# Hyena's chain on the vector engine alone, and its transforms' first forward and last inverse level summed by TensorE in PSUM

## The chip, the cores and the metric

One core of one Trainium2 chip. The metric is the device time of one execution in microseconds; the kernel before took 2783.18 us, median of three runs (2772.97 to 2788.09).

## The reference

A two-layer trunk over 1,024 tokens of width 1,024 with 256 context tokens, everything in fp32. Layer 0 projects the normalised tokens once and gives the channels to two mixers beside each other: a Hyena operator (512 channels) and a differential attention (four heads); both are joined by one output projection. Layer 1 is a spatial-gating MLP. Each layer ends in a ConvFFN. The change lies in Hyena and, by one table, in the attention's rotary embedding:

```python
def fftconv_bidir(u, h_full, d_skip):
    uf = jnp.fft.rfft(uf32, n=2 * L, axis=1)
    hf = jnp.fft.rfft(h_full, n=2 * L, axis=0)
    y = jnp.fft.irfft(uf * hf[None], n=2 * L, axis=1)[:, :L]
...
    v, x1, x2 = jnp.split(proj, 3, axis=-1)
    z = v
    for o, gate in enumerate((x1, x2)):
        z = gate * fftconv_bidir(z, filt[:, o], d_skip[o])
```

So there are two long convolutions one after the other, each a transform, a product with the filter's spectrum and an inverse transform, and a gate behind it.

## The kernel before

`layer0_front` holds two generators that `eager` interleaves. `main` makes the projections, a tile of 128 channels by 1,024 tokens at a time: V (`proj_v`), the context's K (`proj_kc`), Hyena's twelve tiles with the short convolution (`proj_hyena`, `conv_mtile`), and the eight tiles of Q and K with their rotation (`proj_qk`). Each such tile is 48 fp32r products of 512 columns, from weights that are split into a rounded part (`whi`, ScalarE) and a rest (`wlo`, `wunit`); the table `F_W` says which engine makes the rest. `side` makes the filters' spectra (`filters`, `dft_part`, written to `Hd`) and then, for each half of 256 channels, the chain of `conv_chain`: for o = 0 and 1, `dft`, `spectrum`, `idft`, and the inverse products with the gate. That makes four rounds in a row; each needs the result of the one before it in its half, and the second half comes behind the first.

A round: `dft(z, n)` multiplies the eight residues of time (slots 0 to 7, in two groups of four) with cosine and sine tables (`tbf`) on TensorE; `fwd(z, c, g)` is four fp32 products of 256 columns into one two-bank PSUM tile (`pf`, two buffers). Group 1 is copied to SBUF by ScalarE (L437), then VectorE forms sum and difference with group 0 straight from PSUM (`a`, `b`). The other levels of the transform are additions of 256, 512 or 1,024 elements per partition in f8 tiles, and two scaled ones (`stt`). `spectrum` multiplies with the filter's spectra, loaded from `Hd` into h8 tiles by DMAs on ScalarE's queue (L314). `idft` adds up again, in place, into E and O, and its last level makes q0 and q1 from E plus and minus O. The inverse products with `tbi` follow: for o = 0, 16 products of 256 columns in two tiles, each multiplied by the gate x1 into the next z; for o = 1, 32 products of 128 columns, multiplied by x2 and stored to `yd`.

Which engine takes an addition is written in tables of letters, V for VectorE (DVE in the profile), G for GpSimd (POOL): `F_DFT` (18 letters a round), `F_INV` (25), `F_SP` (6 for each half spectrum), `F_ROPE` (4 for each Q or K tile: two multiplications, an addition, a subtraction), `F_PART` for the filters. `turns` deals them out in the program's order. The lines of all these additions are L132 (`binop`) and L128 (`stt`), so the profile's rows tell them apart by tile: f is an f8 tile, h a loaded spectrum or a late Q or K, t a t4 tile (a projection's result, four buffers), pj the projections' PSUM, pf Hyena's.

The order in which each engine's queue gets its instructions is set by the tile framework's scheduler when the program is built, from the program's order, priorities (`first()` puts evacuations ahead) and its own estimates. Each queue then runs in order, and an instruction that waits holds up those behind it.

Of the kernel before, what the change touches and what calls it, by code (L numbers as in the profile page):

```python
# [20 lines left out]
P = 128  # L21
# [16 lines left out]
UL, UP = (10, 8, 10), ((6,) * 7,) * 3  # L38
DL, DP = (1, 5, 4, 4, 5), ((3, 3, 3, 3, 3, 5, 8),) + ((3,) * 7,) * 4
BW, LW = 6, 2  # L40
F_DFT, F_INV = ("VGVGVVVGVVVGVGVVVG", "VGVGVVVGVVVGVGVVVG", "VGVGVVVGVVVGVGVVVG", "VGVGVVVGVVVGGGVVVG"), ("VGVVVVGGVGVVVGGGVVGVGVVGG", "VGVVVVGGVGVVVGGGVVGVGVVGG", "VGVVVVGGVGVVVGGGVVGVGVVGG", "VGVVVVGVVGVVVGGGVVGVGVVGG")
F_PART = ("VGGGVGGVVVVVG", "VGGVVGGVVVVVV", "VGGGVGGVVVVVG", "VGGVVGGVVVVVV", "VGGGVGGVVVVVG", "VGGVVGGVVVVVV", "VGGGVGGVVVVVG", "VGGVVGGVVVVVV")
F_SP = ("GGVVVV", "GGVVVV", "GGVVVV", "GGVVVV", "GGVVVV", "GGVVVV", "GGVVVV", "GGVVVV")
F_W = ("GGGGGGGGGGGG", "GGGG", "VGGG", "VGGVVGGG")
F_ROPE = ("GVVG", "GVVV", "GVVG", "VVVG", "GVVG", "GVVG", "GVVV", "GVGG")
F_H, F_X, F_SQ = "VGVVGVVG", "VVVVVVVV", ("V", "V", "V", "V", "V", "V", "V")
A_D = "GGGGGGGGGGGGGGGGGGGGGGGVGVGGVGGVV"
A_C = "VAV" * 4
# [22 lines left out]
RT2 = math.sqrt(0.5)  # L71
# [21 lines left out]
def tile_kernel(ctx: ExitStack, tc: tile.TileContext, ap: dict, out: bass.AP, stop=None):  # L93
# [194 lines left out]
    def layer0_front(fp):  # L288
        with ExitStack() as es:
# [141 lines left out]
            def dft(z, n):  # L431

                e = turns(F_DFT[n])
                a, b = f8(), f8()
                for c in range(2):
                    g1 = fwd(z, c, 1)
                    A.copy(out=b[:, c], in_=g1)  # L437
                    g0 = fwd(z, c, 0)
                    add(V, a[:, c], g0, b[:, c])
                    sub(V, b[:, c], g0, b[:, c])  # L440
                    yield
                cd = f8()
                add(e(), cd[:, :, 0:2], a[:, :, 0:2], a[:, :, 2:4])
                sub(e(), cd[:, :, 2:4], a[:, :, 0:2], a[:, :, 2:4])
                Xe = f8()
                add(e(), Xe[:, :, 0], cd[:, :, 0], cd[:, :, 1])
                sub(e(), Xe[:, :, 2], cd[:, :, 0], cd[:, :, 1])
                sub(e(), Xe[:, 0, 1], cd[:, 0, 2], cd[:, 1, 3])
                add(e(), Xe[:, 1, 1], cd[:, 1, 2], cd[:, 0, 3])
                add(e(), Xe[:, 0, 3], cd[:, 0, 2], cd[:, 1, 3])  # L450
                sub(e(), Xe[:, 1, 3], cd[:, 1, 2], cd[:, 0, 3])
                yield
                eu = f8()
                sub(e(), eu[:, 0, 0], b[:, 0, 0], b[:, 1, 2])
                add(e(), eu[:, 1, 0], b[:, 1, 0], b[:, 0, 2])
                add(e(), eu[:, 0, 1], b[:, 0, 0], b[:, 1, 2])
                sub(e(), eu[:, 1, 1], b[:, 1, 0], b[:, 0, 2])
                sub(e(), eu[:, :, 2], b[:, :, 1], b[:, :, 3])
                add(e(), eu[:, :, 3], b[:, :, 1], b[:, :, 3])
                uv = f8()  # L460
                sub(e(), uv[:, 0, 0], eu[:, 0, 2], eu[:, 1, 3])
                add(e(), uv[:, 1, 0], eu[:, 1, 2], eu[:, 0, 3])
                add(e(), uv[:, 0, 1], eu[:, 0, 2], eu[:, 1, 3])
                sub(e(), uv[:, 1, 1], eu[:, 1, 2], eu[:, 0, 3])
                Xo = f8()
                stt(V, Xo[:, :, 0:2], uv[:, :, 0:2], RT2, eu[:, :, 0:2], MUL, ADD)
                stt(V, Xo[:, :, 2:4], uv[:, :, 0:2], -RT2, eu[:, :, 0:2], MUL, ADD)
                return Xe, Xo
# [102 lines left out]

            def idft(Y, n):

                ye, yo = Y
                e = turns(F_INV[n])
                t = f8()
# [23 lines left out]
                sub(e(), O[:, 0, 3], d[:, 1, 1], d[:, 0, 1])  # L600
                stt(V, O[:, 1, 3], d[:, 0, 1], -1.0, d[:, 1, 1], MUL, SUB)
                yield
                q0, q1 = f8(), f8()
                add(e(), q0[:, :, 0], E[:, :, 0], O[:, :, 0])
                sub(e(), q1[:, :, 0], E[:, :, 0], O[:, :, 0])
                stt(V, q0[:, :, 1::2], O[:, :, 1::2], RT2, E[:, :, 1::2], MUL, ADD)
                stt(V, q1[:, :, 1::2], O[:, :, 1::2], -RT2, E[:, :, 1::2], MUL, ADD)
                add(e(), q0[:, 0, 2], E[:, 0, 2], O[:, 1, 2])
                sub(e(), q0[:, 1, 2], E[:, 1, 2], O[:, 0, 2])
                sub(e(), q1[:, 0, 2], E[:, 0, 2], O[:, 1, 2])  # L610
                add(e(), q1[:, 1, 2], E[:, 1, 2], O[:, 0, 2])
                return q0, q1

            def conv_chain(half):
                while half not in zs:
# [2 lines left out]
                for o in range(2):  # L618
# [7 lines left out]
                    if o == 0:  # L626
                        xg = h8(x1d[half].rearrange("p a b -> p (a b)"), (1, 8))[:, 0]
                        z = f8z()
                        for g in range(2):
                            ps = ps4()  # L630
                            for r in range(4):
                                for c in range(2):
                                    mm(ps[:, r], tbi[:, c, g * 4 + r], q[g][:, c, r], c == 0, c == 1)
                            gs = slice(g * 4, g * 4 + 4)
                            mul(V, z[:, gs], ps, xg[:, gs])
                            yield
                    else:
                        for j in range(2):
                            ps = ps2("pf")
                            for g in range(2):  # L640
                                for r in range(4):
                                    rs = slice((g * 4 + r) * P, (g * 4 + r + 1) * P)
                                    for c in range(2):
                                        mm(ps[:, rs], q[g][:, c, r, j * P : (j + 1) * P], tbi[:, c, g * 4 + r],
                                           c == 0, c == 1)
                            t = t4()
                            st(t, x2d[2 * half + j])
                            tv = t.rearrange("p (s r) -> p s r", r=8)
# [1225 lines left out]
```

## Time and profile before

| | us |
|---|---|
| median of three runs | 2783.18 |
| lowest, highest | 2772.97, 2788.09 |
| the profiled execution | 2781.85 |
| its span, first to last instruction | 2780.1 |
| TensorE busy (share of the span) | 2488.7 (90%) |
| VectorE busy | 1803.7 (65%) |
| GpSimd busy | 1264.8 (45%) |
| ScalarE busy | 1205.2 (43%) |

The profiled execution's own time is the span and 1.75 us around it. The shares are averages over stages that differ. Hyena's chain lies between 289 and 601 us of the span, attention begins at 663, and the rest of the network follows it. An fp32 product (the Hyena ones) appears as two records on TensorE; an fp32r product as one. Records of TensorE overlap in the timeline, so its pace is read from one start to the next.

### The profile page before, as it was taken

What the parts mean: (1) busy time and instruction counts of PE and PEld (TensorE: products, weight loads), DVE (VectorE), ACT (ScalarE), POOL (GpSimd) and SP (SyncE); (2) the same over time, 40 slices, a digit from 0 to 9 for tenths busy, and PEclk for the clock granted to TensorE, in tenths of its full rate; (3) what the DMA queues carried; (4) which work ended last, traced back from release to release, by engine and by line L of the source; (5) the groups of instructions that cost most, each with busy time, mean ns of one, the idle gap of its engine ahead of it and who ended that gap; (6) DMA issues with size and microseconds to landing.
All of it is one profiled execution on the core that took longest, in us unless ns stands there. A gap on an engine that the chain in (4) does not pass through costs nothing. (4 is left out here: it accounts for less than half of the span.)

```text
span 2780.1 us, 30586 instructions
## 1 busy us (share of the span) xinstructions
PE 2488.7 (90%) x11192; PEld 1981.5 (71%) x11192; DVE 1803.7 (65%) x2021; ACT 1205.2 (43%) x1871; POOL 1264.8 (45%) x917
## 2 busy tenths in 40 slices
PE   6799667767988889999999999999999999999897
PEld 2798556655767766777777777778877777787676
DVE  4676787874998376656666876642367665566854
ACT  2322111113767255555555444512257565665342
POOL 1333654545444163332323776613343433338775
PEclk9899888888999989999999999999999999999998
DMA  7134131235761265788878833311335777779422
GB/s 279 65 111 158 38 121 39 90 128 181 227 188 50 73 204 129 206 206 216 217 205 227 294 121 110 113 38 48 142 88 125 175 181 170 173 160 319 144 80 99
DMA packets 166855, 412.76 MB, mean 148 GB/s; under 512 B 16011, under 2 KB 28815, under 8 KB 164528
## 3 DMA queue, kind: packets, MB, share of 16 engines
q1 hardware_dynamic: 86352, 248.76, 27.9%
q0 software_dynamic: 34848, 63.45, 13.4%
q10 hardware_dynamic: 45504, 98.58, 9.6%
q8 instruction: 88, 1.44, 0.2%
q14 instruction: 63, 0.52, 0.1%
HBM read 261.31 MB, written 85.98 MB: 125 GB/s over the span
## 5 line engine op out<-in xcount | busy, mean ns | idle before, releaser
L154 PE MATMUL b<-u,u 128*128 128x512 f32 (+1 forms) x5624 | 1331.1, 396 | 65.2 <-POOL u L132 23.8
L154 PEld LDWEIGHTS b<-u,u 128*128 128x128 f32 x5624 | 1063.1, 192 | 331.4 <-POOL u L132 34.1
L132 DVE TENSOR_TENSOR u<-u,u 128x512 fp32r<-128x512 f32 (+2 forms) x470 | 464.5, 1014 | 337.9 <-ACT u L1141 178.9
L132 POOL TENSOR_TENSOR u<-u,u 128x512 fp32r<-128x512 f32 (+1 forms) x338 | 504.6, 1514 | 298.5 <-ACT u L1141 183.9
L1152 POOL DMA_DIRECT2D u<-u x242 | 211.3, 920 | 491.9 <-ACT u L1151 378.7
L1141 ACT CAST u<-u 128x512 fp32r<-128x512 f32 x462 | 261.7, 616 | 238.6 <-DVE u L132 96.0
L154 PE MATMUL b<-x,u 128*128 128x512 f32 x1224 | 296.8, 397 | 0.8 <-DMA u<-u 0.8
L128 DVE SCALAR_TENSOR_TENSOR u<-u,cols,u 128x1023 f32<-128x1023 f32 x176 | 232.3, 1326 | 93.2 <-ACT u L1588 85.2
L154 PEld LDWEIGHTS b<-x,u 128*128 128x128 f32 x1224 | 229.5, 188 | 61.9 <-issue 3.4
L132 POOL TENSOR_TENSOR f<-f 128x256 f32<-128x256 f32 (+2 forms) x99 | 124.7, 1273 | 209.9 <-DVE f L132 180.7
L1150 ACT CAST u<-u 128x512 fp32r<-128x512 f32 x242 | 146.1, 614 | 117.7 <-DVE u L132 89.6
L1151 ACT ACTIVATE u<-u 128x512 fp32r<-128x512 f32 x242 | 149.3, 628 | 67.2 <-POOL u L132 60.3
L132 DVE TENSOR_TENSOR f<-f 128x256 f32<-128x256 f32 (+3 forms) x176 | 177.2, 1055 | 1.1
L132 DVE TENSOR_TENSOR u<-u,b 128x512 f32<-128x512 f32 (+1 forms) x132 | 112.2, 859 | 71.5 <-PE b L154 66.7
L154 PE MATMUL pj<-hh,whi 128*128 128x512 f32 x320 | 132.7, 415 | 24.2 <-DVE t L128 14.0
L1588 ACT ACTIVATE u<-u,cols 128x1024 f32<-128x1024 f32 x88 | 109.3, 1242 | 90.2 <-DVE u L132 89.4
L128 DVE SCALAR_TENSOR_TENSOR x<-b,mods,x 128x512 f32<-128x512 f32 (+1 forms) x104 | 88.7, 905 | 68.4 <-PE b L154 68.4
L154 PE MATMUL pj<-hh,wlo 128*128 128x512 f32 x320 | 130.2, 407 | 3.2 <-POOL wlo L132 1.6
L154 PE MATMUL pj<-hl,whi 128*128 128x512 f32 x320 | 131.3, 410 | 0.0
L132 POOL TENSOR_TENSOR p<-p,p 128x1280 f32<-128x1280 f32 x27 | 79.4, 2944 | 94.1 <-ACT p L885 75.3
L874 ACT ACTIVATE p<-s,nx 128x1280 f32<-128x1280 f32 x64 | 85.0, 1328 | 42.0 <-DVE nx L870 39.2
L147 ACT CAST whi<-wraw 128x1024 fp32r<-128x1024 f32 x28 | 29.3, 1049 | 160.5 <-PE pj L154 138.5
(229 smaller groups left out, 3218.3 us busy)
## 6 DMA issues: line engine op xcount, KB each, us to landing
u<-u POOLq DMA_DIRECT2D x242, 256.0 KB, 4.6
u<-wup SPq DMA_DIRECT2D x88, 512.0 KB, 4.9
Td<-u ACTq DMA_DIRECT2D x66, 512.0 KB, 5.5
u<-Td SPq DMA_DIRECT2D x56, 512.0 KB, 4.4
wraw<-modw SPq DMA_DIRECT2D x48, 512.0 KB, 5.5
u<-wdown SPq DMA_DIRECT2D x40, 512.0 KB, 6.1
wraw<-modw0b SPq DMA_DIRECT2D x32, 512.0 KB, 4.6
xs<-x ACTq DMA_DIRECT2D x48, 256.0 KB, 2.0
```

The source lines that it names most:

```text
L128: eng.scalar_tensor_tensor(out=o, in0=a, scalar=sc, in1=b, op0=op0, op1=op1)
L132: eng.tensor_tensor(out=o, in0=a, in1=b, op=op)
L147: A.copy(out=hi, in_=x)
L154: T.matmul(o, l, r, start=st and not onto, stop=sp, skip_group_check=onto)
L874: A.activation(q.p[m], q.s, AF.Exp, bias=q.nx, accum_out=q.l[:, m : m + 1])
L1141: A.copy(out=t[:, H0], in_=x)
L1150: A.copy(out=t[:, H0], in_=x)
L1151: A.activation(t[:, H1], t[:, H0].bitcast(F32), AF.Copy, scale=-1.0)
L1152: G.dma_start(out=t[:, H1], in_=x, accum_op=ADD)
L1588: A.activation(a, c, AF.Identity, bias=col(f"fb{l}", f), scale=col(f"fw{l}1", f))
```

## The change

All letters of `F_DFT`, `F_INV`, `F_SP` and `F_ROPE` become V. The first level of `dft` is no longer made by VectorE: each sum and each difference of the two groups is accumulated in a PSUM tile by two products per residue, the difference with a copy of z's second group that ScalarE negates (`zn`, a t4 tile); ScalarE then copies all four tiles to SBUF. The last level of `idft` goes the same way: instead of q0 and q1 ScalarE makes a negated copy `n` of O (slots 1 and 3 scaled by the root of one half) and scales O's slots 1 and 3 in place, and each inverse product becomes two, one with E and one with O or n.

```diff
-F_DFT, F_INV = ("VGVGVVVGVVVGVGVVVG", ...
+F_DFT, F_INV = ("V" * 18,) * 4, ("V" * 25,) * 4
-F_SP = ("GGVVVV", ...
+F_SP = ("V" * 6,) * 8
-F_ROPE = ("GVVG", "GVVV", "GVVG", "VVVG", "GVVG", "GVVG", "GVVV", "GVGG")
+F_ROPE = ("VVVV",) * 8
...
                 a, b = f8(), f8()
+                zn = t4().rearrange("p (r n) -> p r n", r=4)
+                A.activation(zn, z[:, 4:8], AF.Copy, scale=-1.0)
                 for c in range(2):
-                    g1 = fwd(z, c, 1)
-                    A.copy(out=b[:, c], in_=g1)
-                    g0 = fwd(z, c, 0)
-                    add(V, a[:, c], g0, b[:, c])
-                    sub(V, b[:, c], g0, b[:, c])
+                    for o, z1 in ((a, z[:, 4:8]), (b, zn)):
+                        ps = ps4()
+                        for r in range(4):
+                            mm(ps[:, r], tbf[:, c, r], z[:, r], True, False)
+                            mm(ps[:, r], tbf[:, c, 4 + r], z1[:, r], False, True)
+                        A.copy(out=o[:, c], in_=ps)
...
-                q0, q1 = f8(), f8()
-                add(e(), q0[:, :, 0], E[:, :, 0], O[:, :, 0])
-                sub(e(), q1[:, :, 0], E[:, :, 0], O[:, :, 0])
-                stt(V, q0[:, :, 1::2], O[:, :, 1::2], RT2, E[:, :, 1::2], MUL, ADD)
-                stt(V, q1[:, :, 1::2], O[:, :, 1::2], -RT2, E[:, :, 1::2], MUL, ADD)
-                add(e(), q0[:, 0, 2], E[:, 0, 2], O[:, 1, 2])
-                sub(e(), q0[:, 1, 2], E[:, 1, 2], O[:, 0, 2])
-                sub(e(), q1[:, 0, 2], E[:, 0, 2], O[:, 1, 2])
-                add(e(), q1[:, 1, 2], E[:, 1, 2], O[:, 0, 2])
-                return q0, q1
+                n = f8()
+                for r, w in ((0, 1.0), (1, RT2)):
+                    A.activation(n[:, :, r::2], O[:, :, r::2], AF.Copy, scale=-w)
+                A.activation(O[:, :, 1::2], O[:, :, 1::2], AF.Copy, scale=RT2)
+
+                def terms(g, c, r):
+                    if r == 2:
+                        o = (O, n)[g ^ c][:, 1 - c, 2]
+                    else:
+                        o = (O, n)[g][:, c, r]
+                    return E[:, c, r], o
+
+                return terms
...
-                                    mm(ps[:, r], tbi[:, c, g * 4 + r], q[g][:, c, r], c == 0, c == 1)
+                                    for i, x in enumerate(q(g, c, r)):
+                                        mm(ps[:, r], tbi[:, c, g * 4 + r], x, c + i == 0, c + i == 2)
```

The products of the second order change in the same way.

The change moves instructions between engines and, through the scheduler, in their queues. POOL's queue in the first round, before: f8 are the chain's tiles, h8 the loaded spectra, wlo the rests of the projections' weights.

```order
L132 TENSOR_TENSOR f8_240_1910<-f8_233_1873 128x256
L132 TENSOR_TENSOR f8_240_1910<-f8_233_1873 128x2x256
L132 TENSOR_TENSOR f8_241_1917<-f8_240_1910 128x256
L132 TENSOR_TENSOR f8_244_1927<-f8_239_1903,h8_243_1925 128x1024 x2
L132 TENSOR_TENSOR f8_247_1937<-f8_242_1922,h8_246_1935 128x1024
L132 TENSOR_TENSOR wlo_296_2252<-wraw_294_2249,whi_295_2251 128x1024
L132 TENSOR_TENSOR f8_247_1937<-f8_242_1922,h8_246_1935 128x1024
L132 TENSOR_TENSOR f8_249_1945<-f8_239_1903 128x2x512
L132 TENSOR_TENSOR f8_239_1903<-f8_249_1945 128x256 x2
L132 TENSOR_TENSOR f8_250_1954<-f8_242_1922 128x2x512
L132 TENSOR_TENSOR wlo_301_2312<-wraw_299_2309,whi_300_2311 128x1024
```

And with the change, the same stretch of POOL's queue and what comes next on it:

```order
L132 TENSOR_TENSOR wlo_263_2062<-wraw_261_2059,whi_262_2061 128x1024
L132 TENSOR_TENSOR wlo_296_2288<-wraw_294_2285,whi_295_2287 128x1024
L132 TENSOR_TENSOR wlo_301_2348<-wraw_299_2345,whi_300_2347 128x1024
L132 TENSOR_TENSOR wlo_310_2482<-wraw_308_2479,whi_309_2481 128x1024
L132 TENSOR_TENSOR wlo_317_2552<-wraw_315_2549,whi_316_2551 128x1024
```

The chain's part has gone to VectorE's queue; between the chain's begin and its end only the weight rests of projection tiles are left, one of them for each tile whose letter in `F_W` is G.

TensorE's queue around the inverse products of the second round (pf_304 and pf_306, second order of the first half), before; pj_318 is the projection tile that lies around them, and the transposes of the next half's z (line 682) stand behind its last product, 32 of its products behind the last row of pf_306:

```order
L154 MATMUL pj_318_2487<-hh4_363,wlo_317_2484 128x512
L154 MATMUL pj_318_2487<-hh5_369,whi_316_2483 128x512
L154 MATMUL pf_304_2369<-tbi_110,f8_292_2239 128x128 x4
L154 MATMUL pf_304_2369<-tbi_110,f8_293_2240 128x128 x8
L154 MATMUL pf_306_2390<-tbi_110,f8_292_2239 128x128 x4
L154 MATMUL pf_306_2390<-tbi_110,f8_293_2240 128x128 x8
L154 MATMUL pj_318_2487<-hl5_370,whi_316_2483 128x512
L154 MATMUL pj_318_2487<-hh5_369,wlo_317_2484 128x512
L154 MATMUL pj_318_2487<-hh6_375,whi_316_2483 128x512
L154 MATMUL pj_318_2487<-hl6_376,whi_316_2483 128x512
```

And with the change, where the block alternates between E (f8_280) and O or n (f8_283, f8_293):

```order
L154 MATMUL pf_306_2442<-tbi_110,f8_293_2281 128x128
L154 MATMUL pf_306_2442<-tbi_110,f8_280_2216 128x128
L154 MATMUL pf_306_2442<-tbi_110,f8_283_2235 128x128
L154 MATMUL pf_306_2442<-tbi_110,f8_280_2216 128x128
L154 MATMUL pf_306_2442<-tbi_110,f8_293_2281 128x128
L154 MATMUL pf_306_2442<-tbi_110,f8_280_2216 128x128
L154 MATMUL pf_306_2442<-tbi_110,f8_293_2281 128x128
L154 MATMUL pj_318_2555<-hh7_381,whi_316_2551 128x512
L154 MATMUL pj_318_2555<-hl7_382,whi_316_2551 128x512
L154 MATMUL pj_318_2555<-hh7_381,wlo_317_2552 128x512
L691 MATMUL pj_320_2608<-ident_62,t4_312_2534 128x128 x8
```

The block now has 54 of its 64 products in a row at this place, and 3 of the projection's 48 products behind it where there were 32; the others have moved ahead of it. In the last round 8 such products behind the block have become none. In the first and third round, 21 of the 32 products stand together at the end, behind ScalarE's copies.

## Rows read from the trace of the kernel before

**Rows 1.** Busy time by stretch: PE, PEld, DVE, ACT, POOL (records), clock, DMA

```profile
289.00:601.00 312.00, 213.59 (x938) 176.69 (x939) 261.11 (x206) 37.31 (x37) 176.80 (x95) 0.83 0.22 75
601.00:674.50 73.50, 60.16 (x255) 48.00 (x253) 31.13 (x27) 17.13 (x17) 39.50 (x15) 0.93 0.58 187
```

**Rows 2.** TensorE's waits, 289 to 601 us: for whom, total, times, longest

```profile
PE pf L154 <- DVE f L132: 55.8, 4, 23.1
```

**Rows 3.** TensorE's timeline: start, duration, operation, count, idle before and what ended it

```profile
289.08 5.45 PE L154 MATMUL pf<-f,tbf 128*128 128x256 f32 x24 [2.06 <-ACT f L734]
...
352.50 9.23 PE L154 MATMUL pf<-f,tbi 128*128 128x256 f32 x32 [15.80 <-DVE f L132]
...
445.46 1.05 PE L682 MATMUL pj<-ident,t 128*128 128x128 f32 x8
...
595.18 5.74 PE L154 MATMUL pf<-tbi,f 128*128 128x128 f32 x48
...
604.60 0.50 PE L154 MATMUL pj<-hh,whi 128*128 128x512 f32 x1 [1.83 <-ACT t L773]
...
663.26 1.30 PE L154 MATMUL s<-f,f 128*128 128x512 f32 x6
674.47 2.08 PE L154 MATMUL s<-f,f 128*128 128x512 f32 x4 [9.90 <-ACT t L773]
```

**Rows 4.** DVE's timeline, single operations at 350 to 362 and 402 to 408 us

```profile
349.70 0.94 DVE L128 SCALAR_TENSOR_TENSOR f<-f 128x256 f32<-128x256 f32 x1
...
351.76 0.68 DVE L132 TENSOR_TENSOR f<-f,f 128x512 f32<-128x512 f32 x1
352.36 2.35 DVE L128 SCALAR_TENSOR_TENSOR f<-f,f 128x1024 f32<-128x1024 f32 x2
354.63 0.74 DVE L132 TENSOR_TENSOR f<-f,f 128x256 f32<-128x256 f32 x2
...
361.77 1.22 DVE L132 TENSOR_TENSOR f<-pf,h 128x1024 f32<-128x1024 f32 x1 [1.36 <-PE pf L154]
...
402.81 2.17 DVE L132 TENSOR_TENSOR f<-f 128x1024 f32<-128x1024 f32 x1
404.90 1.27 DVE L128 SCALAR_TENSOR_TENSOR t<-pj,cols,t 128x1023 f32<-128x1023 f32 x1
406.10 1.21 DVE L132 TENSOR_TENSOR f<-f 128x1024 f32<-128x1024 f32 x1
407.23 1.21 DVE L132 TENSOR_TENSOR f<-f,h 128x1024 f32<-128x1024 f32 x1
```

**Rows 5.** POOL's timeline: a weight split with DVE still, and one beside DVE

```profile
287.10 2.35 POOL L132 TENSOR_TENSOR wlo<-wraw,whi 128x1024 fp32r<-128x1024 f32 x1 [13.40 <-ACT whi L147]
...
320.65 3.33 POOL L132 TENSOR_TENSOR wlo<-wraw,whi 128x1024 fp32r<-128x1024 f32 x1
```

**Rows 6.** DVE's timeline: begin and end of its work between the products, each round

```profile
300.02 12.79 DVE L132 TENSOR_TENSOR f<-f 128x1024 f32<-128x1024 f32 x12
...
374.14 6.14 DVE L132 TENSOR_TENSOR f<-f 128x1024 f32<-128x1024 f32 x3
...
432.12 0.75 DVE L132 TENSOR_TENSOR f<-f,f 128x256 f32<-128x256 f32 x2
...
461.19 12.88 DVE L132 TENSOR_TENSOR f<-f 128x1024 f32<-128x1024 f32 x12
...
515.93 0.74 DVE L132 TENSOR_TENSOR f<-f,f 128x256 f32<-128x256 f32 x2
...
535.00 2.46 DVE L132 TENSOR_TENSOR f<-f 128x1024 f32<-128x1024 f32 x1
...
592.03 0.75 DVE L132 TENSOR_TENSOR f<-f,f 128x256 f32<-128x256 f32 x2
```

**Rows 7.** ScalarE's timeline before the scores: a cast of Q or K, an evacuation

```profile
669.53 1.04 ACT L779 CAST h<-t 128x1024 fp32r<-128x1024 f32 x1 [7.25 <-POOL t L132]
673.39 1.02 ACT L773 ACTIVATE t<-pj 128x1024 f32<-128x1024 f32 x1 [2.82 <-DMA Kd<-h]
```

More of the change, by code (lines that the diff above doesn't have):

```diff
@@ L40 @@
 BW, LW = 6, 2
-F_DFT, F_INV = ("VGVGVVVGVVVGVGVVVG", "VGVGVVVGVVVGVGVVVG", "VGVGVVVGVVVGVGVVVG", "VGVGVVVGVVVGGGVVVG"), ("VGVVVVGGVGVVVGGGVVGVGVVGG", "VGVVVVGGVGVVVGGGVVGVGVVGG", "VGVVVVGGVGVVVGGGVVGVGVVGG", "VGVVVVGVVGVVVGGGVVGVGVVGG")
+F_DFT, F_INV = ("V" * 18,) * 4, ("V" * 25,) * 4
 F_PART = ("VGGGVGGVVVVVG", "VGGVVGGVVVVVV", "VGGGVGGVVVVVG", "VGGVVGGVVVVVV", "VGGGVGGVVVVVG", "VGGVVGGVVVVVV", "VGGGVGGVVVVVG", "VGGVVGGVVVVVV")
-F_SP = ("GGVVVV", "GGVVVV", "GGVVVV", "GGVVVV", "GGVVVV", "GGVVVV", "GGVVVV", "GGVVVV")
+F_SP = ("V" * 6,) * 8
 F_W = ("GGGGGGGGGGGG", "GGGG", "VGGG", "VGGVVGGG")
-F_ROPE = ("GVVG", "GVVV", "GVVG", "VVVG", "GVVG", "GVVG", "GVVV", "GVGG")
+F_ROPE = ("VVVV",) * 8
 F_H, F_X, F_SQ = "VGVVGVVG", "VVVVVVVV", ("V", "V", "V", "V", "V", "V", "V")
@@ L643, in conv_chain @@
                                     for c in range(2):
-                                        mm(ps[:, rs], q[g][:, c, r, j * P : (j + 1) * P], tbi[:, c, g * 4 + r],
-                                           c == 0, c == 1)
+                                        for i, x in enumerate(q(g, c, r)):
+                                            mm(ps[:, rs], x[:, j * P : (j + 1) * P], tbi[:, c, g * 4 + r],
+                                               c + i == 0, c + i == 2)
                             t = t4()
```

## The prediction

> **What bounds the kernel now.** I read the stretches first [rows 1]. From 289 to 601 us TensorE is busy 213.6 of 312 us at a granted clock of 0.83, DVE 261.1; POOL, which takes the "G" turns of the same chain, 176.8. So in this stretch DVE runs nearly all the time and TensorE stands idle for 98 us; see both there. Then the list of TensorE's waits [rows 2]: 55.8 us in four waits of the Hyena products (pf) for DVE's f tiles: one before the inverse products of each of the chain's four rounds (two halves by two orders). Then TensorE's timeline [rows 3]: a round starts with the forward products (289.08) and ends with the inverse ones (352.50 in the first, 595.18 in the last), each behind a stall of 15.80 or 23.11 us. Behind the last stand five projection tiles and the scores (663.26), whose third bank waits 9.90 us. So the end of this stage is set by a chain: forward products, DVE and POOL, inverse products, four times.
>
> Why is DVE so slow? A 1,024-element operation on SBUF takes 2.17 us at 402.81 and 1.21 at 406.10 [rows 4]; POOL was at work during the first and idle during the second. POOL pays too: its split lasts 2.35 us when DVE is still and 3.33 beside it [rows 5]. Work shared by the two is done twice as slowly by one of them, and each waits for the other's part.
>
> **The change, part by part.** Prices on DVE with POOL still are steps from one start to the next [rows 4]: 1.13 us for 1,024 elements (406.10 to 407.23), 0.60 for 512 (351.76), 0.35 for 256 (half of 0.74 at 354.63, less overlap), 0.87 for the small scalar one (349.70), 1.14 for a large one (half of 2.35 less overlap), 1.20 for one that reads PSUM (404.90).
>
> *DVE's chain.* It keeps, per round: of the forward transform 2 of 1,024, 4 of 512, 12 of 256 and 2 large scalar ones, 11.2; of the spectrum 12 of 1,024, 13.7; of the inverse 4 of 1,024, 4 of 512, 11 of 256 and a small scalar one, 11.7; in all 36.5 us. Between them stand the short convolution's operations: 4, 6, 4 and 2 of 1.20 in the four rounds, and in the last two splits and a shuffle of 3.7. POOL keeps the weight splits: its order has nothing else here, and 9 fall on the chain (2, 3, 2, 2). While one lasts, 3.33 us, DVE does 3.33/2.09 operations worth 1.13 each, so it loses 1.5, say 1.6. That gives 44.5 + 48.5 + 44.5 + 45.8 = 183 us. Before, from the first operation behind the forward sums to the last before the products [rows 6]: 300.02 to 355.37 (354.63 + 0.74 [rows 4]), 374.14 to 432.87, 461.19 to 516.67, 535.00 to 592.78: 227. **Gain 44.**
>
> The Trainium skill (SBUF — State Buffer, "Who interferes with whom") says that the pair of ports which DVE and POOL share is locked for a whole instruction and the second comer waits fully. The rows show less than that: both stretch, 2.35 to 3.33 and 1.21 to 2.17. By the rule each of the nine splits could cost DVE 2.35 instead of 1.6, 7 us more, and the forecast would be 2764.
>
> *Forward products.* Each sum now has two products, so 64 records for 32, 0.227 us each (5.45 for 24 at 289.08 [rows 3]). DVE can start behind the third of four banks: 48 x 0.227 + a ScalarE copy of 1.02 (673.39 [rows 7]) + 0.2 = 12.1 us, against 289.08 to 300.02 = 10.9 with DVE's own sums. **Costs 1.2 x 4 = 5.** The negated copy is one ScalarE operation beside the first bank: nothing, since only the second bank reads it; without that cover 1.0 a round.
>
> *Last inverse level.* DVE loses eight operations (they lie in the 44), ScalarE gains three scaled copies of about 1.0 each; two of them follow DVE's last operation: 2.4 with the hand-overs. The products double, and by the order 21 of 32 (first order), 54 of 64 (second) stand behind these copies. A product is two records: 0.46 us for 256 columns, 0.24 for 128 (5.74 for 48 records at 595.18). First order, two rounds: 2.4 + about 24 x 0.46 (the 21 and what is left of the five before) + DVE's multiplication 1.3 = 14.7, against 355.37 to 362.99 (361.77 + 1.22 [rows 4]) = 7.6: +7.2 each. Second round: the order moves 29 of the 32 projection products that stood behind the inverse block to before it, into a stall. Before, 432.87 to the transposes at 445.46 = 12.6; after, 2.4 + 54 x 0.24 + 3 x 0.23 = 16: +3.4. Last round: 592.78 to 602.77 (604.60 less its wait [rows 3]) = 10.0; after, 15.9 as eight products go ahead: +5.9. **Costs 24.**
>
> The added instructions on TensorE are some 62 us of work (32 records more in each forward block and first-order block, 64 in a second-order one). What I don't charge lies in the 98 us of idleness; without that cover the 62 would be paid in full. ScalarE was busy 37 of these 312 us [rows 1], but its queue is in order: the copies stand behind loads of spectra that wait for buffers. In the order, one such load now stands behind the negated copy, which needs z; I cost that at nothing because its reader is DVE some 25 us later.
>
> *Rotary on DVE alone.* After the chain come five projection tiles. Before, 602.77 to the third scores at 674.47 = 71.7 us [rows 3]; of that, 9.90 is a wait for ScalarE's evacuation at 673.39, which stood behind a cast at 669.53 that had waited 7.25 us for POOL's rotary addition [rows 7]. On DVE the rotation is four of 1.13 behind a shuffle, under 6 us of a tile's 11.7 (58.7 from 604.60 to 663.26, five tiles), so the last evacuation should follow its products by some 2 us. Bounds: 0, if DVE's queue, where these operations stand behind the chain's last multiplications, holds them up as long; 11.7, both waits gone. I take 8, nearest the second since the row names POOL. **Gain 8.**
>
> Sum: -44 + 5 + 24 - 8, with the decimals -23.5 us, on the profiled execution's 2781.85 us: **2758 us**. The median of the three runs, 2783.18, lies 1.3 above that execution, well within the runs' spread; I leave it there. What follows (attention, the rest of the network) is unchanged and starts that much earlier; the stage behind waits on no clock of its own.
>
> **The rivals.**
> *TensorE takes it back.* The inverse blocks run behind a stall at the pace of 352.50, 9.23 us for 32 records (0.288), not 0.227, which adds some 7 us to all four, and the rotation saves nothing: -24 + 8 + 7 = -9, 2773 us, no change that can be told. For it: the clock of 0.83 [rows 1] and the order of DVE's queue; against: TensorE's waits shrink. 0.15.
>
> *Slower: the products at the lower clock.* TensorE's two levels are 1.2 and 2.4 GHz; the 0.83 is a mix of them. Were the inverse products behind ScalarE's copies wholly at the lower one, they would cost 2 x 24 x 0.46 + 2 x 54 x 0.24 = 48 us more: 2758 + 48 = 2806. It decides once half of them run so (+24). Against it: 48 records in 5.74 at 595.18, right behind the longest stall, are at the full level, only the first few of 352.50 are not. 0.05. The Trainium skill (TensorE: Matmul & The Clock Gate, Part 1) makes the lower clock the state into which idleness puts TensorE; the trace agrees as far as the first records after a stall.
>
> *The change doesn't do what it says.* DVE's slowness is its own (many short dependent operations) and stays without POOL. Break-even is 24 us over 4 x 36.5: 16% above my prices. At the 2.09 of 402.81 throughout, 4 x 36.5 x 0.85 = 124 us more: 2882. Against it stand the quick rows at 406.10 and 351.76 to 354.63. 0.04.
>
> *More.* The sums' first products, which the order sends ahead, hide most of the inverse blocks (-12), and the rotary wait goes whole (-4): 2742. 0.16.
>
> **How the numbers follow.** My forecast has 0.60, the rivals 0.15, 0.05, 0.04 and 0.16. A measurement of this kernel tells some 0.5%, 14 us, from no change, so the bounds are 2769 and 2797. Faster: 0.60 + 0.16 = 0.76; same: 0.15; slower: 0.09. The range reaches from the larger gain, 2740, to beyond the first rival, 2779; the slower cases and the tails, under 2 in 10, are left out. Unknown costs inside it: the splits (7), the rotation (-4 to +8), the blocks' pace (7).
>
> **What would show it.** DVE's 1,024-element operations of the chain at 1.2 us, not 1.8 to 2.1; POOL with only splits between 289 and the chain's end; forward blocks of 64 records in 14.5 us; the last inverse block ending near 585, not 601; the third scores near 650, not 674; the rest earlier by as much. Wrong would be: DVE operations above 1.35 us on average, inverse blocks above 17 us, stalls on ScalarE's copies, or a gain at 650 us that is gone at the end.

## The result and the profile after

| | before | after |
|---|---|---|
| median, us | 2781.65 | 2748.24 |
| lowest, highest | 2772.97, 2788.09 | 2745.12, 2750.17 |
| the profiled execution | 2781.85 | 2747.28 |
| its span | 2780.1 | 2745.5 |

Four runs each, the three shown ahead of the prediction among those of before. The ratio is 0.9881, with an interval of 0.9852 to 0.991: faster by 33 us, where 2758 was forecast (a gain of 24), inside the range of 2740 to 2779.

The page's busy times of the kernel after, and its two stretches:

```profile
PE 2528.8 (92%) x11512; PEld 2024.1 (74%) x11512; DVE 1757.6 (64%) x2071; ACT 1229.7 (45%) x1895; POOL 1103.9 (40%) x819
```

```profile
289.00:601.00 312.00, 279.79 (x1346) 237.74 (x1347) 215.17 (x260) 69.53 (x68) 48.72 (x11) 0.95 0.28 94
601.00:674.50 73.50, 62.31 (x280) 50.43 (x278) 57.12 (x62) 34.93 (x42) 17.24 (x6) 0.93 0.73 227
```

Against [rows 1]: in the same 312 us TensorE is busy 279.8 instead of 213.6 (it has the added products, and what follows the chain has moved in), its granted clock is 0.95 for 0.83, and POOL does 48.7 us of work where it did 176.8.

VectorE's operations of the chain by form, 289 to 601 us; first the kernel before, then after (busy us, then mean ns of one):

```profile
L132 DVE TENSOR_TENSOR f<-f 128x256 f32<-128x256 f32 x57 | 53.5, 983 | 0.3
L132 DVE TENSOR_TENSOR f<-f 128x1024 f32<-128x1024 f32 x28 | 51.0, 1846 | 0.0
L132 DVE TENSOR_TENSOR f<-f 128x512 f32<-128x512 f32 x23 | 33.4, 1471 | 0.0
L132 DVE TENSOR_TENSOR f<-f,h 128x1024 f32<-128x1024 f32 x16 | 32.9, 2088 | 0.0
```

```profile
L132 DVE TENSOR_TENSOR f<-f 128x1024 f32<-128x1024 f32 x40 | 47.9, 1240 | 44.4 <-ACT f L443 44.4
L132 DVE TENSOR_TENSOR f<-f,h 128x1024 f32<-128x1024 f32 x32 | 43.7, 1420 | 0.0
L132 DVE TENSOR_TENSOR f<-f 128x256 f32<-128x256 f32 x92 | 34.2, 437 | 0.1
L132 DVE TENSOR_TENSOR f<-f 128x512 f32<-128x512 f32 x32 | 26.9, 877 | 0.1
```

More operations, and less time: 92 of 256 elements now take 34.2 us where 57 took 53.5. The first line's idle 44.4 us are the four waits for ScalarE's copy of the forward sums.

TensorE's timeline after, at the same places as [rows 3]: the first forward block, the first inverse block behind ScalarE's copies, the second half's transposes, the last inverse block, what follows it, and the second and third tiles of scores (six products each):

```profile
289.86 4.15 PE L154 MATMUL pf<-f,tbf 128*128 128x256 f32 x18 [2.06 <-ACT f L743]
...
348.16 11.38 PE L154 MATMUL pf<-f,tbi 128*128 128x256 f32 x52
...
435.37 1.05 PE L691 MATMUL pj<-ident,t 128*128 128x128 f32 x8
...
569.09 13.67 PE L154 MATMUL pf<-tbi,f 128*128 128x128 f32 x108 [4.02 <-ACT f L610]
582.52 0.47 PE L154 MATMUL pj<-hh,whi 128*128 128x512 f32 x1
...
638.39 1.42 PE L154 MATMUL s<-f,f 128*128 128x512 f32 x6
...
642.59 1.65 PE L154 MATMUL s<-f,f 128*128 128x512 f32 x6 [2.78 <-ACT p L883]
```

What the prediction calls the third scores, at 674.47 before, is the second tile: its first begins at 663.26 and has the first six products. After the change the second tile begins at 638.39 and waits for nothing. The 2.78 us at 642.59 are the third tile's wait for attention's own exponent (p); before, that tile waited 1.76 us for the same.

ScalarE's second scaled copy at the end of the first round, behind which the 52 records at 348.16 stand:

```profile
346.71 1.06 ACT L610 ACTIVATE f<-f 128x1024 f32<-128x1024 f32 x1
```

VectorE's at the end of the first and second rounds, and the begin of the third:

```profile
345.17 0.42 DVE L128 SCALAR_TENSOR_TENSOR f<-f 128x256 f32<-128x256 f32 x1
...
359.58 1.23 DVE L132 TENSOR_TENSOR f<-pf,h 128x1024 f32<-128x1024 f32 x1 [3.09 <-PE pf L154]
...
419.85 0.42 DVE L128 SCALAR_TENSOR_TENSOR f<-f 128x256 f32<-128x256 f32 x1
...
451.87 1.22 DVE L132 TENSOR_TENSOR f<-f 128x1024 f32<-128x1024 f32 x1 [11.71 <-ACT f L443]
```

VectorE finishes its first round at 345.59 (before, 355.37), but z is ready only at 360.81 (before, 362.99): 15.2 us behind it instead of 7.6.

The stretch up to the second tile of scores can be cut at the same events in every kernel. The last column is the first experiment below, which has the tables of letters without the sums.

| us, over the four rounds | before | after | forecast of after - before | after - before | letters alone |
|---|---|---|---|---|---|
| begin of the first forward products | 289.1 | 289.9 | 0 | +0.8 | 287.9 |
| forward products to VectorE's first operation | 45.8 | 47.8 | +5 | +1.9 | 46.5 |
| VectorE's part | 227.3 | 182.3 | -44 | -45.1 | 201.2 |
| VectorE's end to z, or to the block's end | 40.5 | 62.6 | +24 | +22.1 | 16.1 |
| last block to the second tile of scores | 71.7 | 55.9 | -8 | -15.8 | 62.6 |
| second tile of scores at | 674.5 | 638.4 | -23 | -36.1 | 614.3 |

(In the second round the cut behind VectorE's end is the next half's first forward product.) The whole 36.1 us last until the 13th tile of scores (36.0); at the 16th, 685.31 for 715.70, 30.4 are left. In between TensorE's transposes of attention's p wait twice for VectorE, 2.18 and 2.23 us, where before they waited 0.44 in all. The span gained 34.6 in the end, 1.5 less than the second tile.

### The profile page after: what moved, and what is told of

Same layout as the page of the kernel before. It is cut to its first block, busy times and chain, and to the rows that moved or that the text cites. A ratio compares the mean times of both kernels' runs of the same rounds, so it can differ in the third digit from the quotient of the medians.

```text
span 2745.5 us, 31122 instructions
## 1 busy us (share of the span) xinstructions
PE 2528.8 (92%) x11512; PEld 2024.1 (74%) x11512; DVE 1757.6 (64%) x2071; ACT 1229.7 (45%) x1895; POOL 1103.9 (40%) x819
## 5 line engine op out<-in xcount | busy, mean ns | idle before, releaser
L132 POOL TENSOR_TENSOR wlo<-wraw,whi 128x1024 fp32r<-128x1024 f32 x24 | 82.2, 3428 | 322.5 <-ACT whi L147 239.7
L132 DVE TENSOR_TENSOR f<-f 128x256 f32<-128x256 f32 (+3 forms) x232 | 148.6, 699 | 45.5 <-ACT f L443 44.4
L154 PE MATMUL pf<-f,tbf 128*128 128x256 f32 x416 | 101.8, 387 | 7.3 <-ACT f L743 4.1
```

Of the source, the lines that this page charges most:

```text
L132: eng.tensor_tensor(out=o, in0=a, in1=b, op=op)
L154: T.matmul(o, l, r, start=st and not onto, stop=sp, skip_group_check=onto)
```

## The experiments

Medians, each against the kernel before on the same chip (its medians there are 2780.4 to 2781.7 us):

| kernel | us | ratio, 95% interval |
|---|---|---|
| the change | 2748.2 | 0.9852 to 0.991 |
| letters alone | 2724.1 | 0.976 to 0.9823 |
| TensorE's sums alone | 2800.6 | 1.0045 to 1.0102 |
| change, rotation's letters as before | 2755.3 | 0.9871 to 0.9937 |
| change, weight rests on VectorE | 2720.4 | 0.9729 to 0.9806 |
| letters and forward sums | 2729.8 | 0.9794 to 0.983 |
| letters and inverse sums | 2735.3 | 0.9816 to 0.9866 |
| rests on VectorE, POOL adds in a scratch tile | 2764.7 | 0.992 to 0.9955 |
| rests on VectorE, POOL sets a scratch tile | 2720.5 | 0.9766 to 0.9806 |
| change, z's transposes early | 2744.1 | 0.9844 to 0.9883 |
| letters, rests on VectorE | 2714.7 | 0.9746 to 0.978 |
| the same with forward sums | 2715.9 | 0.9746 to 0.9783 |

### The change in two halves

Letters alone keeps `fwd`, the `add` and `sub` behind it and q0, q1 as they were; the sums alone deal out the old letters, the last six of each inverse string unused.

```diff
-F_DFT, F_INV = ("VGVGVVVGVVVGVGVVVG", ...
+F_DFT, F_INV = ("V" * 18,) * 4, ("V" * 25,) * 4
-F_SP = ("GGVVVV", ...
+F_SP = ("V" * 6,) * 8
-F_ROPE = ("GVVG", ...
+F_ROPE = ("VVVV",) * 8
```

These lines on the kernel before are the letters alone; taken back on the kernel after they leave the sums alone.

> The letters alone: all of the chain's additions and the rotation on DVE, the first forward and last inverse level as before (sums and differences on DVE, single products on TensorE). Theory (what pays is that POOL no longer works beside DVE): per round DVE has 4.9 us more than with the whole change, but the inverse block and the forward block cost what they did before, so four rounds give -45 + 20 of DVE's time, nothing for the products, and -9 at the rotation's tail: -34, about 2748 us, the same as the whole change within 8 us. Rival (TensorE's summing is what pays): the gain shrinks to the rotation and a part of the chain, 2765 us or more.

> TensorE's sums alone, with the old letters. Theory: DVE loses its last level (about 5.5 us a round at the old pace, 22 in all), the inverse blocks cost 20 more, the forward blocks 2: within 8 us of the kernel before, 2782. Rival (TensorE's summing is what pays): 2765 us or less. A second rival (the summing costs by itself, its products and copies on the chain's path): 2795 or more.

On the letters alone theory and rival both missed: 2724, a gain of 57 us. On the sums alone the theory (2782) and the first rival missed too, and the second rival came true: the summing costs by itself. The letters are worth more without the sums than with them, and the sums cost 24 us with the new letters (2748.2 less 2724.1) and 19.5 with the old ones (2800.6 less 2781.1). TensorE's timeline of the letters alone shows where; the inverse blocks of the first, second and last rounds, the forward products behind the first two, and the second tile of scores:

```profile
346.74 2.87 PE L154 MATMUL pf<-f,tbi 128*128 128x256 f32 x12 [1.42 <-DVE f L132]
349.68 4.52 PE L154 MATMUL pf<-f,tbi 128*128 128x256 f32 x20
355.66 2.54 PE L154 MATMUL pf<-f,tbf 128*128 128x256 f32 x11
...
411.89 9.78 PE L154 MATMUL pf<-tbi,f 128*128 128x128 f32 x64 [10.79 <-DVE f L132]
421.51 1.68 PE L154 MATMUL pf<-f,tbf 128*128 128x256 f32 x7
...
542.31 9.40 PE L154 MATMUL pf<-tbi,f 128*128 128x128 f32 x64 [25.11 <-DVE f L132]
...
614.26 2.21 PE L154 MATMUL s<-f,f 128*128 128x512 f32 x6 [2.50 <-ACT t L773]
```

And VectorE's last operations of the first and second rounds there:

```profile
349.49 1.42 DVE L132 TENSOR_TENSOR f<-f,f 128x256 f32<-128x256 f32 x4
...
414.63 1.42 DVE L132 TENSOR_TENSOR f<-f,f 128x256 f32<-128x256 f32 x4
```

The inverse products begin at 346.74, 4.2 us ahead of VectorE's end at 350.91, and at 411.89 against 416.05: they run into its last level, group after group, at 0.226 us a record (4.52 for 20). Before the change the first block also began ahead of VectorE's end, by 2.9 us (352.50 against 355.37), but behind a stall of 15.80 us, and its 32 records took 9.23 us; now they take 7.46. In the second round the next half's forward products follow at 421.51, 5.5 us behind VectorE, where it was 15.7 before: 32 projection products and the transposes no longer stand between. With the sums nothing like it is possible, since n and the scaled O are copies of VectorE's last result: the 52 records at 348.16 of the kernel after all stand behind them. So taking the last level off VectorE, with the first forward one, saves about 19 us on it (201.2 less 182.3) and costs 46.5 behind it (62.6 less 16.1). In the first round 3.3 us of products are left behind VectorE's end with the letters alone; with the sums it is 2.6 us until the copies are done and then a block of 11.38. How much of that is the doubled number of products and how much the lost overlap no run separates.

### The rotation

```diff
-F_ROPE = ("VVVV",) * 8
+F_ROPE = ("GVVG", "GVVV", "GVVG", "VVVG", "GVVG", "GVVG", "GVVV", "GVGG")
```

> The whole change without the rotation's letters. Theory: the chain keeps its gain, the stretch from the last inverse block to the third scores goes back from 62 us to about 71: 2757 us. Rival (the rotation gave nothing by itself, the tail shortened because the chain's end freed the queues): 2748 us.

2755.3, 7 us above the change, near the theory's 2757. The slowest run of the change (2750.2) is below the fastest of this kernel (2752.2), but the two intervals of the ratio overlap, so the size is a rough one. The trace shows more at the place itself; TensorE's line of the second tile of scores:

```profile
651.59 2.50 PE L154 MATMUL s<-f,f 128*128 128x512 f32 x6 [9.90 <-ACT t L782]
```

The wait of 9.90 us is back, and the stretch from the last inverse block is 69.6 us (expected, about 71) where the change has 55.9: 13.7 longer. At the 16th tile of scores 7.5 of it are left.

### Which of the two sums costs

Two kernels with all letters V. On the letters alone the first has this, and no hunk in `idft` and `conv_chain`; the second has those and not this:

```diff
-                    g1 = fwd(z, c, 1)
...
+                            mm(ps[:, r], tbf[:, c, r], z[:, r], True, False)
+                            mm(ps[:, r], tbf[:, c, 4 + r], z1[:, r], False, True)
```

> All letters V and the first forward level summed by TensorE; the last inverse level on VectorE as before. The letters alone took 2724.1, the whole change 2748.2, so the two sums together cost 24. Theory: it is the inverse level that costs (+19.8 over its four blocks against +2.0 over the forward blocks in the traces), so this is 2724 + 2 to 5 = 2726 to 2729. Rival: the cost is not in the blocks but in the order that the scheduler makes once TensorE's queue is longer (the next half's transposes no longer ahead of the second round's inverse block); then either sum alone brings it and this is 2738 or more.

> All letters V and the last inverse level summed by TensorE; the first forward level on VectorE as before. Theory (the inverse blocks cost): 2724 + 20 = 2744, with 2740 to 2748. Rival (the forward sums cost through the order): 2724 to 2730 here and 2738 or more with the forward sums alone.

2729.8 and 2735.3. The first is just above the theory's 2726 to 2729. The second missed 2740 to 2748 by 5, but the begin of attention in its trace comes near the theory's size: the second tile of scores begins at 629.73 us, 15.5 behind that of the letters alone (614.26); with the forward sums alone at 616.36, 2.1 behind. TensorE's timeline of the two at that place, forward sums first:

```profile
616.36 2.19 PE L154 MATMUL s<-f,f 128*128 128x512 f32 x6 [2.47 <-ACT t L776]
```

```profile
629.73 1.43 PE L154 MATMUL s<-f,f 128*128 128x512 f32 x6
```

The profiled execution of the inverse kernel, 2729.7, is the fastest of its four. Its lag holds until about 2,200 us and is mostly made up by 2,460, in code that is the same; I don't know by what. With both sums the second tile of scores is 24.1 behind, as much as the medians differ, and 6.6 more than 2.1 and 15.5. These 6.6 us lie between VectorE's end and z or the block's end, 62.6 us with both sums and 55.9 with the inverse ones alone. I took this for the order of TensorE's queue and tried it.

```diff
                     if kind == 0:
+                        with first():
+                            ps = to_time(a)
+                    else:
+                        ps = to_time(a)
```

> The whole change with the eight transposes of each tile of z given the priority of the evacuations; in TensorE's queue those of the second half then stand ahead of the first half's last inverse block instead of behind it. Theory (part of what the two sums cost together, some 6 us beyond 2 for the forward and 16 for the inverse level, is this order, because the next half's forward products wait for the transposes and ScalarE's copy): the distance from the first half's last chain operation on VectorE to the next forward products, 18 us with the change, falls by 4 to 7, and the time is 2741 to 2745. Rival (the products themselves are the cost, 108 records at this place): the transposes only take the products' place, 2747 to 2750.

The time, 2744.1, is in the theory's interval, but 4 us are within both kernels' spread, and the mechanism failed. TensorE's timeline of this kernel, and VectorE's end of the second round:

```profile
417.42 1.05 PE L691 MATMUL pj<-ident,t 128*128 128x128 f32 x8
420.82 12.22 PE L154 MATMUL pf<-tbi,f 128*128 128x128 f32 x108
434.93 4.05 PE L154 MATMUL pf<-f,tbf 128*128 128x256 f32 x18
```

```profile
416.70 0.42 DVE L128 SCALAR_TENSOR_TENSOR f<-f 128x256 f32<-128x256 f32 x1
```

The transposes have moved ahead of the block, and still the forward products begin 17.8 us behind VectorE's end (417.12 to 434.93) where it was 18.2: the 108 records are what is waited for. The 6.6 us of the two sums together are left open.

### POOL beside VectorE

The change left one kind of work on POOL in the chain, the weight rests. This kernel gives those of the Hyena tiles and of Q and K to VectorE:

```diff
-F_W = ("GGGGGGGGGGGG", "GGGG", "VGGG", "VGGVVGGG")
+F_W = ("VVVVVVVVVVVV", "GGGG", "VGGG", "VVVVVVVV")
```

> The whole change, and the weight splits of Hyena's and of the Q and K tiles on DVE too, so that POOL does nothing beside the chain. Theory (a split on POOL costs DVE about 1.6 us): nine times 1.6 are saved and nine times 1.14 spent, -4 us: 2744. Rival by the lock that holds a whole instruction: nine times 2.35 saved, -11: 2737. Rival on the other side (splits in DVE's queue come late for the projections): 2750 or more.

All missed: 2720.4, 28 us below the change. Its VectorE rows, 289 to 601 us:

```profile
L132 DVE TENSOR_TENSOR f<-f,h 128x1024 f32<-128x1024 f32 x32 | 37.5, 1220 | 0.0
L132 DVE TENSOR_TENSOR f<-f 128x256 f32<-128x256 f32 x92 | 32.2, 418 | 0.1
L132 DVE TENSOR_TENSOR f<-f 128x512 f32<-128x512 f32 x32 | 20.7, 686 | 0.1
```

Against the rows of after these three are shorter by 14.4 us. VectorE's part of the four rounds is 10.7 shorter (171.6 us), though seven of the added rests lie in it; four operations of the short convolution, 4.8 us, moved out of it. The chain begins 3.4 earlier, and the blocks between VectorE's parts are 6.8 shorter; with the tail (0.1) that makes 20.8 us at the second tile of scores. At the 16th tile it is 27.5, about what the medians differ by (27.9).

Was it VectorE's slowing, or were the products waiting for POOL's rests? In the trace of after TensorE waits for no result of POOL between 280 and 645 us. To settle it, two kernels put work on POOL whose result nobody needs, at the places of the 20 rests: `dum` is a scratch tile, and a copy of one element on VectorE ties it to its place. That copy must wait until POOL has finished the set before.

```diff
+        if extra:
+            V.tensor_copy(out=dum[:, 0:1], in_=h[:, 0:1])
+            for _ in range(8):
+                add(G, dum, dum, dum)
...
+            for _ in range(16):
+                G.memset(dum, 0.5)
```

> The change with all weight rests made by VectorE (2720.4), and at each of the 20 places of the first twelve and last eight projection tiles eight additions of 384 elements on POOL that read and write a scratch tile nobody needs. Nothing waits for POOL here. Theory (POOL's reading of SBUF takes time from VectorE's operations beside it): a set is 8 x 0.88 = 7 us of POOL alone (2.35 us for 1,024), VectorE loses 4.6 to 7 us per set, some ten sets fall on the chain and about seven tenths of them beside VectorE: 32 to 50 us, so 2752 to 2770. Rival (the rests on POOL cost because TensorE's projections waited for them, not because of VectorE's slowing): 2720 to 2726.

> As the run with POOL's scratch additions, but sixteen memsets of the same scratch tile in their place: POOL is busy at the same places and writes SBUF but reads none. Theory (reading is what collides): 2720 to 2726. Rival (any work of POOL on SBUF slows VectorE): most of what the scratch additions cost, 2740 or more.

The upper kernel has the additions, the lower (from its `for` on) the memsets. 2764.7 and 2720.5: the theory on both sides. TensorE's and ScalarE's queues of the two kernels are the same, instruction by instruction. One place of VectorE's and POOL's timelines, the first round's last nine additions; with POOL's additions:

```profile
345.89 8.68 DVE L134 TENSOR_TENSOR f<-f 128x512 f32<-128x512 f32 x9
```

```profile
346.00 8.29 POOL L134 TENSOR_TENSOR dum<-dum 128x384 f32<-128x384 f32 x8 [44.74 <-DVE dum L197]
355.05 7.14 POOL L134 TENSOR_TENSOR dum<-dum 128x384 f32<-128x384 f32 x8 [0.76 <-DVE dum L197]
```

With the memsets:

```profile
337.32 3.64 DVE L134 TENSOR_TENSOR f<-f 128x512 f32<-128x512 f32 x9
```

```profile
337.40 7.55 POOL L199 MEMSET dum<- 128x384 f32 x16 [42.90 <-DVE dum L197]
```

The same nine operations take 8.68 us beside additions and 3.64 beside memsets. VectorE loses 5.04 us to POOL work of 7.14 (its length with VectorE still), and POOL itself 1.15. Over the chain VectorE is busy 219.1 us with the additions, 196.5 with the memsets and 194.5 with neither, and 1.9 of the memsets' 2.1 are the small copies (the first two rows have the same 269 records of VectorE):

```profile
293.60:595.70 302.10, 264.20 (x1279) 225.31 (x1280) 219.07 (x269) 63.65 (x62) 97.41 (x104) 0.95 0.25 86
```

```profile
286.40:560.00 273.60, 253.78 (x1246) 216.90 (x1247) 196.54 (x269) 63.85 (x62) 83.25 (x200) 0.98 0.27 92
```

```profile
286.50:560.00 273.50, 253.81 (x1248) 216.99 (x1249) 194.47 (x253) 63.83 (x62) 0.00 (x0) 0.98 0.26 90
```

VectorE's parts of the four rounds are 192.7, 171.6 and 171.6 us long. So reading additions on POOL cost VectorE time here, and work that only writes did not. The small copies did wait for POOL, 14.0 us with the additions and 16.3 with the memsets, none of it inside VectorE's part of a round. The Trainium skill (SBUF — State Buffer, "Who interferes with whom") says this: a VectorE instruction with two inputs in SBUF collides with a POOL instruction that reads SBUF, not with one that only writes. Both runs agree.

Of the 43.3 us between the two profiled executions 21.0 arise in VectorE's four parts, 7.1 ahead of the chain, 2.2 in the blocks, 7.3 in the tail (3.08 of them VectorE's wait for `dum`) and 5.7 behind the second tile of scores. The theory had all of its 32 to 50 us in the chain, from ten sets; about four fell beside VectorE's parts, so its number came out right for more places than it named. A POOL operation that reads one input was not run.

### The best of both

The letters and the rests on VectorE, with the transforms as before the change; and the same with the forward sums.

```diff
+F_DFT, F_INV = ("V" * 18,) * 4, ("V" * 25,) * 4
+F_SP = ("V" * 6,) * 8
+F_ROPE = ("VVVV",) * 8
+F_W = ("VVVVVVVVVVVV", "GGGG", "VGGG", "VVVVVVVV")
```

> All letters V and the weight rests of the twelve Hyena tiles and the eight tiles of Q and K on VectorE too; both levels of the transforms as before the change. The letters alone took 2724.1; with the sums the rests on VectorE gave 28. Theory (POOL's reads cost VectorE's chain, whichever form the levels have): 15 us of slowing in the chain's rows, 3 ahead of it and some behind it are gone, 2698 to 2709. Rival (without the sums VectorE's chain is longer, so that the rests added to it come late): 2718 or more.

> As the run with letters and rests on VectorE, but the first forward level summed by TensorE. Theory (the forward sums cost 2 to 6 by themselves, as in the run without the splits): 2 to 6 above the run without them, 2700 to 2715. Rival (with a shorter chain on VectorE the forward sums pay, since they took 4 us off the first and the third round): 3 or more below it.

2714.7 and 2715.9; 1.2 us is no difference here. Both are 2.4% below the kernel before, and the first 1.2% below the change. Both missed their theories (at most 2709, and 2 to 6 apart). The gain of the rests is only 9 on the letters, not the 15 to 26 expected. In the first kernel's trace the last inverse block ends at 553.56 (543.35 + 10.21), 1.9 us later than with the letters alone (551.71), though its chain begins 3.0 earlier (284.96): in the chain ten rests more on VectorE take back what its operations gain, which is the rival's reason at a smaller price. The 9 us come behind the chain, at the begin of attention: the second tile of scores begins 1.0 us later than with the letters alone, the 13th 2.2 earlier (646.49 for 648.71), the 16th 9.1 earlier (653.77 for 662.86). Between the last two TensorE's transposes wait for VectorE with the letters alone, and don't with the rests moved; what holds VectorE up there was not followed:

```profile
652.61 0.63 PE L892 MATMUL tr<-ident,p 128*128 128x128 f32 x4 [2.18 <-DVE at L901]
...
658.36 0.66 PE L892 MATMUL tr<-ident,p 128*128 128x128 f32 x4 [2.23 <-DVE at L901]
```

The stretch ahead of that, 610.4 to 640, has with the letters alone and then with the rests moved:

```profile
610.40:640.00 29.60, 19.81 (x66) 15.18 (x66) 20.94 (x28) 17.34 (x23) 5.79 (x2) 0.65 0.86 255
```

```profile
610.40:640.00 29.60, 19.90 (x86) 14.90 (x84) 24.95 (x33) 20.34 (x26) 8.72 (x3) 0.88 0.89 254
```

More matmuls (86 for 66) in the same busy time, at a granted clock of 0.88 for 0.65. That bears on what is gained up to the 13th tile, not on the rest. None of this was tried by a run.

## Why the prediction was right, and where only its sum was

**What bounds the kernel: right.** VectorE's part of the four rounds fell from 227.3 to 182.3 us, forecast 183, and the begin of attention and the end moved with it.

**VectorE's slowness is POOL's doing: right, and now shown.** The rival "doesn't do what it says" needed operations 16% above the prediction's prices, and the parts took about 1 us less than these prices add up to. The 1,024-element operations are at 1.24 (from 1.85), those with a loaded spectrum at 1.42 (from 2.09), the 256-element ones at 0.44 (from 0.98). The additions and memsets in a scratch tile, at the same places and with TensorE's and ScalarE's queues alike, show that it is POOL's additions and not its being busy. The price of 1.6 us per rest held in VectorE's rows (14.4 us for the nine that fall on its rounds), and the rival price of 2.35, 21 us, did not; but that was only VectorE's share: with what else moved, the rests cost the whole change 28.

**Forward products: +1.9 for +5.** I let a bank's last product, the copy and 0.2 us follow each other; in three rounds VectorE began 11.3 to 11.7 us behind the products, forecast 12.1, against 10.9 to 11.2 before; in the third, with the projections' short convolution between, 13.4 against 12.6.

**Last inverse level: +22.1 for +24.** By rounds 7.6, 2.5, 6.4 and 5.7, forecast 7.2, 3.4, 7.2 and 5.9. The blocks run at 0.219 us a record (11.38 for 52), so the rival "TensorE takes it back", which wanted 0.288, fell, and the lower-clock rival with it: the granted clock of the stretch rose to 0.95. The reason given against the latter was misread, though: the 48 records at 595.18 are not right behind the longest stall. In front of them stand 16 more of the block, 589.89 to 595.18, at a granted clock of 0.50 (8 records in 2.07 us), which is the lower level, 1.2 GHz. In the last round the prediction's own terms, 2.4 + 54 x 0.24, make 15.4 and not 15.9; 15.7 was measured.

**Rotary: -15.8 for -8 in the tail: the way was right, the size was not.** It lies outside the prediction's own bounds of 0 to 11.7. The wait of the second tile of scores for ScalarE's evacuation (9.90 us) is gone wholly, and so are three others of the tail: 1.83 us for an evacuation, 0.81 and 0.80 for POOL's rests. The third experiment puts 13.7 of the 15.8 on the rotation's letters at that place. But attention gives part of it back, 5.6 us between the 13th and the 16th tile of scores, and 7 us are left in the medians: the size of 8 holds for the end, not for the place that it was worked out for.

So 2758 became 2747.3, the profiled execution: 2.9 us in the forward products, 1.6 in the inverse level, 1.1 in VectorE's part and 7.8 in the tail, less 0.8 for a later begin and less 1.5 that came back behind the second tile of scores. The chain's terms were right within 3 us each, and the one that was clearly mis-sized is the rotation's. "The rest earlier by as much" held for the end only within these 1.5 us, and not on the way there.

Two smaller slips changed nothing. The lock's 7 us on the forecast make 2765, not 2764. And the small scalar operation's price of 0.87 was taken with POOL at work; on the kernel after it takes 0.42 (345.17), some 2 us less over four rounds.

**What the sum hid.** By my terms VectorE drops about 4.9 us a round with the last inverse level (2 x 1.14, 2 x 0.60 and 4 x 0.35), 19.6 of the 44; so the sums should have cost 5 + 24 - 19.6, about 9, and the letters alone should have given 2749. They gave 2724. One share was too small by 25 us, the other too cheap by 15, and the difference, 10, is what the forecast of the whole missed by. The terms were not right by luck, since each was measured by itself, but a sum over the whole could not tell that one half pays and the other costs. I had priced the inverse blocks against those of before, 40.5 us, as if these would stay as they were once POOL was out of the way. They don't: with letters alone they are 16.1 us, since the products then run into VectorE's last level and nothing stands between the halves. In this kernel the change gave up a gain that its other half had just made, and a forecast of the whole change against the kernel before cannot see that.

## What to carry to other kernels

Where a change has two halves, price each against the kernel with the other half in it, not against the kernel before: a wait that the first half removes may be just the cover or the pipeline that the second half spends. In this kernel the chain's last level was best left on the engine whose results come out piece by piece, so that the next engine could start on the first piece; moved behind copies of the chain's very last result, that overlap became a queue, 46.5 us for 19 saved. And POOL work that reads SBUF beside two-input operations of an engine that sets the end cost that engine some two thirds of POOL's own time here, whoever needed its result: 14.4 us for nine rests of 2.35 (21.2 us), 5.04 for additions of 7.14. How far other shapes and operations differ was not run.

## What was unexpected of the hardware

POOL can lose far more than VectorE. Beside VectorE's run of operations POOL's rests of 1,024 elements, 2.35 us with VectorE still, took 7.77 us, and two of them 16.98; POOL's timeline of the kernel after:

```profile
397.98 7.77 POOL L132 TENSOR_TENSOR wlo<-wraw,whi 128x1024 fp32r<-128x1024 f32 x1 [8.12 <-ACT whi L147]
436.50 2.35 POOL L132 TENSOR_TENSOR wlo<-wraw,whi 128x1024 fp32r<-128x1024 f32 x1 [30.75 <-PE pj L691]
...
546.64 16.98 POOL L132 TENSOR_TENSOR wlo<-wraw,whi 128x1024 fp32r<-128x1024 f32 x2 [60.69 <-ACT whi L147]
```

VectorE lost little there: of its operations beside the first of these one is at 2.17 us, the others near their length without POOL. In the run with short additions of 384 elements it was VectorE that lost in the first round, 8.68 us for 3.64, and POOL only 8.29 for 7.14; later in the same run, beside the rotation's operations of 1,024 elements, the same sets on POOL took 9.86 to 10.72 us. So in these runs the side that gave way changed with the operations, and no single factor, as the prediction used, fits both engines.
